# Modulation weights of the first five column blocks loaded in units of two row blocks

## Chip, cores and metric

The kernel runs on one core of a Trainium2 chip. The metric is the device time of one execution in microseconds. Before the change it was 3902.84 us, the median of 3 runs (3902.77 to 3905.11).

## What is computed

Two blocks of a diffusion-like network follow each other on 1024 latent tokens of width 1024, with 256 context tokens. The first block mixes the tokens by a Hyena long convolution and a gated linear recurrence (HGRN2), followed by a mixture of 16 experts. The second has two mixer layers with differential attention. Both blocks scale and shift their normalised inputs by modulation rows, which come from one vector for the latent tokens and one for the context:

```python
s_lat = jax.nn.silu(c)
s_ctx = jax.nn.silu(c_ctx)
sh1, sc1, g1, sh2, sc2, g2 = jnp.split((s_lat @ ada_w[l] + ada_b[l])[:, None, :], 6, axis=-1)
sh1c, sc1c, g1c, sh2c, sc2c, g2c = jnp.split(s_ctx @ ada_w[l] + ada_b[l], 6, axis=-1)
h = modulate(rmsnorm(x, norm1_g[l]), sh1, sc1)
...
shift, scale, gate = jnp.split(jax.nn.silu(c) @ w_mod + b_mod, 3, axis=-1)
shift_c, scale_c, gate_c = jnp.split(jax.nn.silu(c_ctx) @ w_mod + b_mod, 3, axis=-1)
```

So each modulation is a product of 2 rows (the two vectors) with a weight matrix of 1024 rows and 3072 or 6144 columns, all in float32.

## The kernel before

A modulation is made in column blocks of 1024 columns by `mod_rows` (line 306). For one block there are 16 products: 8 row blocks `k` of 128 rows, each in two halves `cb` of 512 columns. A product multiplies the 128x2 vectors (stationary) with a 128x512 piece of weights (moving) and gives 2 rows of 512. The four places `p0 = 64 * (k % 2) + 32 * cb` of one PSUM bank take the products of two neighbouring row blocks; each uses its own 32 columns of the array, so that products in different places can go through side by side. Two additions on VectorE and the bias complete the block. This is done for

- the first two blocks of `ada_w`, in `start` (line 742), ahead of everything that needs a normalised input. Each 128x512 piece is a load of its own (256 KB, lines of 2 KB), in a pool `mr` of 8 buffers;
- the three blocks of `w_mod_2[0]`, in `mods_layer(0)`, which runs beside the streams below with a pool `mr` of 2 such buffers;
- later blocks (`mods_tail`, `mods_layer(1)`) with 128x1024 pieces, which the change leaves as they are.

`start` also normalises the inputs, transposes them (`load_h`, line 399), runs the small network of the filter (`filter_mlp`) and projects the context (`ctx_proj`, line 777), whose weights come in 24 loads to 6 buffers `cr`.

Then `run` (line 1981) lets three streams go side by side. The first is one chain: `filter_time` (line 488; 32 steps, each of 2 matmuls into `pf`, a product with a window `H`, a sum and a difference on VectorE, an absolute value on ScalarE and a sum on GpSimd), `filter_spectra` (line 630) and `hyena` (line 898) with four long convolutions (line 652). One long convolution has 9 bins, each a forward product from `yh`, `yl` and an inverse product from `ph`, `pl`, with DFT constants `dc` that GpSimd loads (line 619). The second stream is `hy_proj` and `hg_proj`: projections of the latent tokens (`T`) with weights from `ar`, split into a high part `ah` (ScalarE) and a low part `al` (GpSimd); 1728 matmuls into `pp`. The third is `mods_layer(0)`. `ctx_state` and `hgrn_head` follow, then the context's part of the second block, the output projection, the choice of tokens and the experts.

The order on each engine isn't that of the code. A scheduler places every instruction by a model of the times, and each engine and each queue of DMAs then works strictly in the order it was given. Loads of all these tiles are issued by SP (line 177), except `dc`. A pool's buffers lie where the pool was opened: pools on one side form a stack, and a pool that is opened after others were closed takes over their space; its first tiles wait for the last readers there.

Of the kernel before, what the change touches and what calls it, by code (L numbers as in the profile page):

```python
# [22 lines left out]
D = 1024  # L23
# [107 lines left out]
class Work:  # L131
# [171 lines left out]
        self.act(s[:, :, 1], b, AF.Silu)  # L303
        return s

    def mod_rows(self, w, bias, c0, ncols, s, rows, pt, tmp, raw, wide=512):

        for b0 in range(c0, c0 + ncols, 1024):
            ps = self.ps(pt)
            for k in range(8):  # L310
                for cb in range(2):
                    if cb * 512 % wide == 0:
                        r = self.t(raw[k % len(raw)] if wide > 512 else raw, [128, wide])
                        self.dma(r, w[k * 128:k * 128 + 128, b0 + cb * 512:b0 + cb * 512 + wide])
                    p0 = 64 * (k % 2) + 32 * cb
                    self.mm(ps[p0:p0 + 2], s[:, k, :], r[:, cb * 512 % wide:cb * 512 % wide + 512], k < 2, k > 5)
            for cb in range(2):
                br = self.t(tmp, [2, 512])
                self.dma(br, bias[b0 + cb * 512:b0 + cb * 512 + 512].partition_broadcast(2))
                self.tt(br, br, ps[32 * cb:32 * cb + 2], ADD)  # L320
                self.tt(br, br, ps[64 + 32 * cb:66 + 32 * cb], ADD)
                self.dma(rows[:, b0 + cb * 512:b0 + cb * 512 + 512], br)
            yield
# [16 lines left out]
        self.m2 = self.dram([2, 2, 3 * D], name="m2")  # L340
        self.A_2, self.sh_2 = [], []

    def mods_layer(self, l, pt, tmp, raw, wide=512):

        I = self.I
        on = self.offb["norm_g_2"]
        yield from self.mod_rows(I["w_mod_2"][l], I["b_mod_2"][l], 0, 3 * D, self.scol2, self.m2[l], pt, tmp, raw, wide)
        mods = self.rows_to_cols(self.m2[l], 0, 16, pt, tmp)
        A = self.cst([128, 2, 8], name="A")
        for i in range(2):  # L350
            self.stt(A[:, i], mods[:, i, 8:16], 1.0, self.cb[:, on + l * 8:on + l * 8 + 8], ADD, MUL)
        self.A_2.append(A)
        self.sh_2.append(mods[:, :, 0:8])

    def mods_tail(self, pt, tmp, raw, wide=512):

        I = self.I
        yield from self.mod_rows(I["ada_w"][0], I["ada_b"][0], 2 * D, 4 * D, self.scol, self.ada, pt, tmp, raw, wide)
        mods = self.rows_to_cols(self.ada, 3 * D, 16, pt, tmp)
        og = self.offs["norm2_g"]  # L360
        self.A2 = self.cst([128, 8], name="A2")
        self.sh2 = mods[:, 0, 0:8]
        self.stt(self.A2, mods[:, 0, 8:16], 1.0, self.ca[:, og:og + 8], ADD, MUL)
# [1603 lines left out]
def side_by_side(*streams):  # L1967

    todo = [[-lead / total, total, list(gens)] for lead, total, gens in streams]
    while todo:  # L1970
        s = min(todo, key=lambda t: t[0])
        g, w = s[2][0]
        if next(g, todo) is todo:
            s[2].pop(0)
            if not s[2]:
                todo.remove(s)
        else:
            s[0] += w / s[1]


def run(K):
    fst = ExitStack()
    with ExitStack() as e1:
        K.open(e1, "left", ar=3, ah=4, al=4)
        K.open_ps(e1, "left", pp=3, mp=1)
        K.open(e1, "left", u2=4, T=16)
        K.open_ps(fst, "right", pf=4)
        K.open(fst, "right", f4=7, fb=5, y=2, t=3, H=2)
        with ExitStack() as e2:
            K.open(e2, "right", cr=6, x=4, c=2, mr=8)  # L1990
            K.start()
        K.open(fst, "right", yh=2, yl=2, ph=2, pl=2, dc=5, ri=7, ra=2, mr=2)
        K.mods_first()
        side_by_side((30, 450, [(K.filter_time(), 2.4), (K.filter_spectra(), 2.1), (K.hyena(), 5)]),
                   (0, 64, [(K.hy_proj(), 1), (K.hg_proj(), 1)]),
                   (0, 4, [(K.mods_layer(0, "mp", "mr", "mr"), 1)]))
    fst.close()
    with ExitStack() as cx:
        with ExitStack() as e1:
            K.open_ps(e1, "left", ph0=3, ph1=3)  # L2000
            K.open(e1, "left", hmk=1, hS=2)
            for p in "01":
                K.open(e1, "left", **{"hi" + p: 6, "hw" + p: 5, "h2" + p: 3, "hm" + p: 4, "hT1" + p: 2, "hT2" + p: 4})
            K.ctx_state()
            for h in range(4):
                K.hgrn_head(h)
            K.open(cx, "right", wr=2, wh=2, wl=2, cu=6, cv=2, Tc=4, lg=2)
            K.pfx = "c"
            with ExitStack() as e2:
                K.open_ps(e2, "right", cp=1, cm=1)  # L2010
                K.open(e2, "right", mr=1)
                for _ in K.mods_tail("cm", "cv", ("wr", "wr", "mr"), 1024):
                    pass
                K.ctx_first()
                K.ctx_side()
                for _ in K.mods_layer(1, "cm", "cv", ("wr", "wr", "mr"), 1024):
                    pass
        K.open_ps(cx, "right", cp=1, cm=1)
        K.pfx = "o"
        em = cx.enter_context(ExitStack())  # L2020
        with ExitStack() as e0:
            K.open_ps(e0, "left", pp=3, pq=2, pi=1)
            with ExitStack() as e1:
                K.open(e1, "left", xm=3, rw=1, wo=16, m4=3, yt=6, u2=3)
                K.out_proj()
            K.open(em, "left", el=4, eh=4, er=10)
            with ExitStack() as e1:
                K.open(e1, "left", twr=2, twh=2, twl=2)
                K.open(e1, "left", aff=1, tk=12, tp=2, af=4)
                K.topk()  # L2030
                K.pfx = "c"
                K.ctx_heads("tw")
        with ExitStack() as e1:
            K.open_ps(e1, "left", et=1, ea=3, ey=2)
            K.open(e1, "right", g2b=1, xg=1, xf=1, xh=4, sa=4, hh=4, yo=2)
            side_by_side((0, 64, [(K.moe(), 1)]), (CL, CT, [(K.ctx_rest(), 1)]))
    K.pfx = ""
    with ExitStack() as e1, ExitStack() as e0, ExitStack() as ec:
        K.open(e0, "right", T0=16)
        rope = K.lat_pools(ec)  # L2040
        hT = K.first_rows()
        K.lat_path(hT, rope, ec, e0, e1)


class Kern:
# [9 lines left out]
    def start(self):  # L2055
        W = self.work
        W.pc, W.psm, W.pd, W.one = self.pc, self.psm, self.pd, self.one
        run(W)
# [119 lines left out]
```

## Time and profile before

| | |
|---|---|
| median of 3 runs | 3902.84 us |
| the profiled execution | 3905.45 us |
| its span | 3903.6 us |
| TensorE busy (matmuls) | 91% |
| VectorE busy | 72% |
| ScalarE busy | 59% |
| GpSimd busy | 31% |
| read from memory, written | 712.65 MB, 107.05 MB |

The span is the time from the first to the last instruction in the profile; 1.85 us of the execution lie around it. Busy shares of the whole span average over stages with different limits, so stretches of the trace are read one by one. Matmuls are pipelined: their busy time counts as one while they overlap, and the start of the next is the better measure of what one costs. A float32 product of 512 columns is recorded as two matmuls.

### The profile page before, as it was taken

The page shows a single profiled execution, that of the slowest core. Times are in us where ns is not written, and L with a number is a line of the kernel's source. Part 1 is how long each engine was busy: PE and PEld are TensorE (multiplying, and loading weights), DVE is VectorE, ACT ScalarE, POOL GpSimd, SP SyncE. Part 2 cuts the span into 40 slices and gives each one's busy share as a digit, 9 for nine tenths or more (in the row PEclk, how much of TensorE's full clock was granted, in tenths as well). Part 3 has the DMA queues.
Part 4 walks back from the last instruction along what each step waited for, and adds up shares of the span by engine and source line. Part 5 has one row for each costly group of instructions (what it writes and reads, how often), then busy time and mean ns, then how long its engine had stood idle before and what let it go on. Part 6 is the DMA issues. An engine that isn't in the chain of part 4 may idle for free. (4 is left out here: it accounts for less than half of the span.)

```text
span 3903.6 us, 52551 instructions
## 1 busy us (share of the span) xinstructions
PE 3554.2 (91%) x17938; PEld 2859.8 (73%) x17938; DVE 2829.5 (72%) x4263; ACT 2290.4 (59%) x3733; POOL 1206.4 (31%) x844
## 2 busy tenths in 40 slices
PE   6999899768897899999999999969989899999989
PEld 2667688646766678787777777768777678877767
DVE  4587778899735788888888888855576744466662
ACT  4444433355434687777777777765566754456772
POOL 3455655454413313221111111001233520133361
PEclk7999999879998999999999999989999999999999
DMA  7767776655376699999999999962311143231133
GB/s 222 228 213 227 224 224 205 220 176 195 103 260 207 197 321 356 322 330 336 361 367 358 363 365 356 362 204 86 111 64 59 49 147 120 74 120 56 41 103 114
DMA packets 529365, 824.25 MB, mean 211 GB/s; under 512 B 38065, under 2 KB 241863, under 8 KB 529096
## 3 DMA queue, kind: packets, MB, share of 16 engines
q1 hardware_dynamic: 502024, 755.74, 56.4%
q0 software_dynamic: 26048, 64.09, 5.9%
q8 instruction: 141, 2.31, 0.2%
q10 hardware_dynamic: 1024, 1.06, 0.1%
q14 instruction: 128, 1.05, 0.1%
HBM read 712.65 MB, written 107.05 MB: 210 GB/s over the span
## 5 line engine op out<-in xcount | busy, mean ns | idle before, releaser
L187 DVE TENSOR_TENSOR el<-er,eh 128x1024 fp32r<-128x1024 f32 x763 | 950.3, 1294 | 113.9 <-ACT eh L184 110.2
L184 ACT ACTIVATE eh<-er 128x1024 fp32r<-128x1024 f32 x768 | 782.9, 1057 | 127.4 <-PE ea L206 92.3
L205 PE MATMUL ea<-el,xh 128*128 128x512 f32 x1024 | 415.5, 406 | 22.7 <-DVE el L187 20.1
L204 PE MATMUL ea<-eh,xh 128*128 128x512 f32 x1024 | 403.7, 397 | 1.0 <-ACT eh L184 0.9
L206 PE MATMUL ea<-eh,xh 128*128 128x512 f32 x1024 | 404.4, 395 | 0.0
L1284 POOL DMA_INDIRECT acc<-yo,idx x16 | 72.0, 4501 | 734.9 <-DVE yo L196 727.9
L1507 DVE TENSOR_SCALAR_CACHE_REDUCE E<-s,rq 128x512 f32<-128x512 f32 (+1 forms) x384 | 237.4, 656 | 82.9 <-PE s L209 75.3
L205 PEld LDWEIGHTS ea<-el,xh 128*128 128x128 f32 x1024 | 192.8, 188 | 91.8 <-DVE el L187 51.3
L181 ACT ACTIVATE E<-E,a 128x1280 f32<-128x1280 f32 x160 | 216.7, 1359 | 64.8 <-DVE a L1511 60.1
L209 PE MATMUL s<-KA,QA 128*128 128x512 f32 (+1 forms) x768 | 213.0, 401 | 33.0 <-DVE E L1507 32.5
L204 PEld LDWEIGHTS ea<-eh,xh 128*128 128x128 f32 x1024 | 192.8, 188 | 46.0 <-ACT eh L184 2.0
L206 PEld LDWEIGHTS ea<-eh,xh 128*128 128x128 f32 x1024 | 193.1, 189 | 37.4
L205 PE MATMUL ey<-el,hh 128*128 128x512 f32 x512 | 207.7, 406 | 4.9 <-DVE el L187 4.7
L204 PE MATMUL ey<-eh,hh 128*128 128x512 f32 x512 | 204.8, 406 | 7.5 <-ACT eh L184 7.5
L206 PE MATMUL ey<-eh,hh 128*128 128x512 f32 x512 | 204.1, 399 | 0.0
L187 POOL TENSOR_TENSOR wl<-wr,wh 128x1024 fp32r<-128x1024 f32 (+1 forms) x48 | 116.1, 2426 | 266.7 <-ACT wh L184 203.7
L209 PEld LDWEIGHTS s<-KA,QA 128*128 128x128 f32 x768 | 134.3, 202 | 76.0 <-DVE E L1507 57.8
L184 ACT ACTIVATE u<-pp 32x512 f32<-32x512 f32 (+2 forms) x212 | 124.4, 587 | 99.7 <-PE pp L206 93.5
L209 PE MATMUL po<-th,V 128*128 128x256 f32 x640 | 168.7, 389 | 15.3 <-ACT th L184 15.3
L204 PE MATMUL pp<-T,ah 128*128 128x512 f32 x448 | 180.8, 403 | 0.0
L205 PE MATMUL pp<-T,ah 128*128 128x512 f32 x448 | 177.8, 397 | 0.0
L206 PE MATMUL pp<-T,al 128*128 128x512 f32 x448 | 177.6, 397 | 0.0
(522 smaller groups left out, 9503.9 us busy)
## 6 DMA issues: line engine op xcount, KB each, us to landing
er<-in_exp_w_dram SPq DMA_DIRECT2D x768, 512.0 KB
wr<-in_w_in_dram SPq DMA_DIRECT2D x60, 512.0 KB
dc<-in_k_dft_dram POOLq DMA_DIRECT2D x72, 384.0 KB, 4.4
dc<-in_k_dft_dram POOLq DMA_DIRECT2D x72, 256.0 KB, 4.2
ar<-in_w_in_dram SPq DMA_DIRECT2D x64, 256.0 KB
mr<-in_w_mod_dram SPq DMA_DIRECT2D x48, 256.0 KB
wr<-in_ada_w_dram SPq DMA_DIRECT2D x24, 512.0 KB
wr<-in_w_out_dram SPq DMA_DIRECT2D x24, 512.0 KB
```

The costliest lines, as they stand in the source:

```text
L181: return self.nc.scalar.activation(out, in_, func, **kw)
L184: return self.nc.scalar.activation(out, in_, AF.Copy)
L187: return (eng or self.nc.vector).tensor_tensor(out, a, b, op=op)
L204: mm(out, lh, rh, start=first, stop=False)
L205: mm(out, lh, rl, start=False, stop=False)
L206: mm(out, ll, rh, start=False, stop=last)
L209: self.nc.tensor.matmul(out, l, r, start=first, stop=last)
L1284: nc.gpsimd.indirect_dma_start(out=self.acc, out_offset=x[0], in_=yo, in_offset=None, compute_op=ADD)
L1507: nc.vector.tensor_scalar(E[:, k0:k1], o, r, None, op0=MUL, op1=ALU.min, accum_out=mx[:, m, j:j + 1] if nc_ > 1 else mc)
```

## The change

In `mod_rows`, two neighbouring row blocks become one load: a tile of 128 x 2 x 1024 elements, 1 MB, with lines of 4 KB, on which four products depend (2 row blocks, 2 halves). The first five column blocks are made this way (`pair=True`): 20 loads instead of 80. Later blocks keep their 128x1024 loads (`pair=False`). The pools change for it: `mr` in `start` has 4 of the large buffers, `mr` beside the streams has one, `dc` has 4 buffers instead of 5, and `y`, `t` and `H`, which `filter_time` uses, are opened after the pools of `start` are closed instead of before.

```diff
-    def mod_rows(self, w, bias, c0, ncols, s, rows, pt, tmp, raw, wide=512):
+    def mod_rows(self, w, bias, c0, ncols, s, rows, pt, tmp, raw, pair=True):
...
             for k in range(8):
+                if not pair:
+                    r = self.t(raw[k % len(raw)])
+                    self.dma(r, w[k * 128:k * 128 + 128, b0:b0 + 1024])
+                elif k % 2 == 0:
+                    r2 = self.t(raw, [128, 2, 1024])
+                    self.dma(r2, w[k * 128:k * 128 + 256, b0:b0 + 1024].rearrange("(k p) n -> p k n", p=128))
+                if pair:
+                    r = r2[:, k % 2]
                 for cb in range(2):
-                    if cb * 512 % wide == 0:
-                        r = self.t(raw[k % len(raw)] if wide > 512 else raw, [128, wide])
-                        self.dma(r, w[k * 128:k * 128 + 128, b0 + cb * 512:b0 + cb * 512 + wide])
                     p0 = 64 * (k % 2) + 32 * cb
-                    self.mm(ps[p0:p0 + 2], s[:, k, :], r[:, cb * 512 % wide:cb * 512 % wide + 512], k < 2, k > 5)
+                    self.mm(ps[p0:p0 + 2], s[:, k, :], r[:, cb * 512:cb * 512 + 512], k < 2, k > 5)
...
-        K.open(fst, "right", f4=7, fb=5, y=2, t=3, H=2)
+        K.open(fst, "right", f4=7, fb=5)
         with ExitStack() as e2:
-            K.open(e2, "right", cr=6, x=4, c=2, mr=8)
+            K.open(e2, "right", cr=6, x=4, c=2, mr=4)
             K.start()
-        K.open(fst, "right", yh=2, yl=2, ph=2, pl=2, dc=5, ri=7, ra=2, mr=2)
+        K.open(fst, "right", y=2, t=3, H=2, yh=2, yl=2, ph=2, pl=2, dc=4, ri=7, ra=2, mr=1)
...
-                for _ in K.mods_tail("cm", "cv", ("wr", "wr", "mr"), 1024):
+                for _ in K.mods_tail("cm", "cv", ("wr", "wr", "mr"), False):
...
-                for _ in K.mods_layer(1, "cm", "cv", ("wr", "wr", "mr"), 1024):
+                for _ in K.mods_layer(1, "cm", "cv", ("wr", "wr", "mr"), False):
```

The schedule changes with it, up to the end of the HGRN2 heads and in a few places behind. Three places on TensorE follow.

The first is in the head, where the last transposes of the first 256 tokens (`x`, the identity `ident`) are followed by the context projection (`cr`, `c`). Before, steps of `filter_time` (from `fb` into `pf`) stand between them:

```order
L209 MATMUL pf_1041<-fb_998,f_99_358 128x512
L209 MATMUL pf_1057<-fb_997,f_99_358 128x512
L209 MATMUL pf_1057<-fb_998,f_99_358 128x512
L212 MATMUL pp_481<-ident_116,x_411 128x128
L212 MATMUL pp_481<-ident_116,x_413 128x128
L209 MATMUL pf_1070<-fb_997,f_99_358 128x512
L209 MATMUL pf_1070<-fb_998,f_99_358 128x512
L209 MATMUL pp_499<-cr_495,c_361 128x128 x4
```

With the change, the same place on TensorE:

```order
L212 MATMUL pp_417<-ident_107,x_354 128x128
L212 MATMUL pp_417<-ident_107,x_356 128x128
L212 MATMUL pp_424<-ident_107,x_354 128x128
L212 MATMUL pp_424<-ident_107,x_356 128x128
L209 MATMUL pp_442<-cr_438,c_304 128x128 x4
```

No filter step is left there; 32 of the 64 matmuls of `filter_time` stood ahead of the first projection matmul, and 8 do now.

The second is the change's place of these 8, right ahead of the first projection (`T` with `ah`), behind the last context unit:

```order
L212 MATMUL pp_887<-ident_107,x_826 128x128
L209 MATMUL pf_956<-fb_949,f_72_301 128x512
L209 MATMUL pf_967<-fb_949,f_72_301 128x512
L209 MATMUL pf_980<-fb_949,f_72_301 128x512
L209 MATMUL pf_993<-fb_949,f_72_301 128x512
L209 MATMUL pf_956<-fb_950,f_72_301 128x512
L212 MATMUL pp_894<-ident_107,x_824 128x128
L212 MATMUL pp_894<-ident_107,x_826 128x128
L209 MATMUL pf_967<-fb_950,f_72_301 128x512
L209 MATMUL pf_980<-fb_950,f_72_301 128x512
L209 MATMUL pf_993<-fb_950,f_72_301 128x512
L204 MATMUL pp_1169<-T_338,ah_1159 128x512
```

These are 4 steps; the other 28 come between the projections. Counted over the whole order, the first inverse product of the first long convolution (`pf` from `ph`) stood behind 1069 projection matmuls and now stands behind 1259; at the last projection matmul three long convolutions were issued, and now two are.

The third shows products of `mods_layer(0)` on TensorE (`mr` with `silu` into `mp`). Before, two of them between units of the context projection:

```order
L209 MATMUL mp_1246<-mr_1253,silu_986 2x512
L209 MATMUL pp_817<-c_361,cr_813 128x256 x4
L209 MATMUL pp_817<-c_362,cr_815 128x256 x4
L209 MATMUL mp_1246<-mr_1256,silu_986 2x512
L209 MATMUL pp_834<-c_361,cr_830 128x256 x4
```

With the change, the third unit, between projections:

```order
L206 MATMUL pp_1169<-T_345,al_1166 128x512
L209 MATMUL mp_1198<-mr_1211,silu_938 2x512 x4
L204 MATMUL pp_1272<-T_338,ah_1159 128x512
L205 MATMUL pp_1272<-T_346,ah_1159 128x512
```

Four products of one unit stand together. That is so for 6 of the 12 units of `mods_layer(0)`; the four products of each of the other 6 are issued in two parts (2 and 2, or 1 and 3) with other work between. Of these 18 groups, 4 stand ahead of the first projection matmul.

## Rows read from the trace of the kernel before

**Rows 1.** The page, busy time of engines: us, share of the span, instructions.
```profile
PE 3554.2 (91%) x17938; PEld 2859.8 (73%) x17938; DVE 2829.5 (72%) x4263; ACT 2290.4 (59%) x3733; POOL 1206.4 (31%) x844
```

**Rows 2.** Busy time by stretches, with granted clock, DMA share and rate.
```profile
core 0: us, PE busy (x) PEld busy (x) DVE busy (x) ACT busy (x) POOL busy (x), PEclk, DMA share, GB/s
0.00:47.00 47.00, 30.25 (x71) 3.46 (x71) 7.13 (x17) 4.14 (x10) 12.10 (x29) 0.75 0.91 284
47.00:81.00 34.00, 17.01 (x50) 10.14 (x51) 22.82 (x38) 28.45 (x59) 8.08 (x7) 0.55 0.40 123
81.00:157.00 76.00, 66.43 (x354) 50.83 (x353) 45.68 (x80) 38.16 (x89) 39.16 (x41) 0.92 0.74 228
157.00:511.00 354.00, 327.44 (x1720) 252.23 (x1721) 279.15 (x410) 143.05 (x302) 198.41 (x182) 0.95 0.74 224
511.00:742.00 231.00, 221.14 (x1215) 192.54 (x1214) 188.06 (x327) 80.01 (x149) 114.72 (x98) 0.98 0.66 210
742.00:804.00 62.00, 29.86 (x171) 26.93 (x170) 60.34 (x116) 21.17 (x49) 30.90 (x37) 0.72 0.71 228
804.00:1024.00 220.00, 166.63 (x1128) 134.17 (x1129) 204.16 (x337) 124.95 (x338) 120.86 (x95) 0.85 0.45 153
1300.00:2400.00 1100.00, 1060.71 (x4895) 850.55 (x4895) 960.42 (x929) 849.97 (x1051) 197.14 (x84) 0.99 0.97 341
```

**Rows 3.** Timeline of TensorE: first and last projections, first inverse product of each convolution.
```profile
156.75 0.80 PE L204 MATMUL pp<-T,ah 128*128 128x512 f32 x1
...
511.19 0.28 PE L204 MATMUL pf<-ph,dc 128*128 128x256 f32 x1
...
597.38 0.28 PE L204 MATMUL pf<-ph,dc 128*128 128x256 f32 x1
...
682.53 0.28 PE L204 MATMUL pf<-ph,dc 128*128 128x256 f32 x1
...
741.60 0.39 PE L205 MATMUL pp<-T,ah 128*128 128x512 f32 x1
741.83 0.39 PE L206 MATMUL pp<-T,al 128*128 128x512 f32 x1
...
768.66 0.41 PE L204 MATMUL pf<-ph,dc 128*128 128x256 f32 x1
```

**Rows 4.** Timeline of TensorE and the view of tile mr (100 to 500, then whole).
```profile
30.10 1.89 PE L209 MATMUL mp<-mr,silu 128*2 128x512 f32 x8
...
136.47 1.02 PE L209 MATMUL mp<-mr,silu 128*2 128x512 f32 x2
137.42 10.63 PE L209 MATMUL pp<-c,cr 128*128 128x256 f32 x48
...
148.19 1.03 PE L209 MATMUL mp<-mr,silu 128*2 128x512 f32 x4
...
L209 PE MATMUL mp<-mr,silu x96: 591/592/1061, 125.7 to 489.5; 128*2 128x512 f32 x96
...
  DMA mr<-in_ada_w_dram: 38.7, 26
```

**Rows 5.** Groups of instructions on VectorE and GpSimd, 0 to 157; one row of ScalarE's timeline.
```profile
L187 DVE TENSOR_TENSOR f<-t 128x256 f32<-128x256 f32 x32 | 20.6, 685 | 0.2
L187 DVE TENSOR_TENSOR t<-pf,H 128x512 f32<-128x512 f32 x16 | 10.8, 682 | 6.2 <-DMA H<-in_k_win_dram 4.2 <-PE pf L209 1.9
...
L187 POOL TENSOR_TENSOR fb<-fb,t 128x512 f32<-128x512 f32 x14 | 18.6, 1327 | 15.6 <-ACT t L181 15.4
...
58.60 1.28 ACT L181 ACT_TABLE_LOAD   x1
```

**Rows 6.** Who waited for whom (us, times, longest): 511 to 742; TensorE 740 to 900.
```profile
POOL dc L621 <- PE pf L206: 62.7, 30, 5.8
...
PE pf L204 <- DMA dc<-in_k_dft_dram: 4.5, 4, 1.4
```

More of the change, by code (lines that the diff above doesn't have):

```diff
@@ L341, in mods_first, with mods_layer @@
         self.A_2, self.sh_2 = [], []
-    def mods_layer(self, l, pt, tmp, raw, wide=512):
+    def mods_layer(self, l, pt, tmp, raw, pair=True):
         I = self.I
         on = self.offb["norm_g_2"]
-        yield from self.mod_rows(I["w_mod_2"][l], I["b_mod_2"][l], 0, 3 * D, self.scol2, self.m2[l], pt, tmp, raw, wide)
+        yield from self.mod_rows(I["w_mod_2"][l], I["b_mod_2"][l], 0, 3 * D, self.scol2, self.m2[l], pt, tmp, raw, pair)
         mods = self.rows_to_cols(self.m2[l], 0, 16, pt, tmp)
@@ L353, in mods_layer, with mods_tail @@
         self.sh_2.append(mods[:, :, 0:8])
-    def mods_tail(self, pt, tmp, raw, wide=512):
+    def mods_tail(self, pt, tmp, raw, pair=True):
         I = self.I
-        yield from self.mod_rows(I["ada_w"][0], I["ada_b"][0], 2 * D, 4 * D, self.scol, self.ada, pt, tmp, raw, wide)
+        yield from self.mod_rows(I["ada_w"][0], I["ada_b"][0], 2 * D, 4 * D, self.scol, self.ada, pt, tmp, raw, pair)
         mods = self.rows_to_cols(self.ada, 3 * D, 16, pt, tmp)
```

## Prediction

> **What bounds the kernel now.** The page's first view gives TensorE 91% and VectorE 72% of the span [rows 1], an average over stages, so I read the busy time by stretches next [rows 2]. The reader should see five regimes ahead of the expert stage, which the change leaves alone. To 47 us the DMA engines are the limit: 91% busy, 284 GB/s, while the first two column blocks (8.39 MB) and early inputs come in. To 81 us ScalarE is, with 28.5 of 34 us. To 157 us TensorE works 66.4 of 76 us on the context projection and the transposes. Then two streams share the engines to 742 us: the projections (1728 matmuls, the first at 156.75 us, the last at 741.83 us [rows 3]) and the filter and Hyena chain. TensorE is 92 to 96% busy there, VectorE only 79 to 81%. From 742 us it turns round: TensorE is down to 48%, VectorE up at 97%, then 93% to 1024 us.
>
> The chain ends this part, since HGRN2's remaining work and everything after waits for its last long convolution. The four convolutions show as first inverse products at 511.19, 597.38, 682.53 and 768.66 us [rows 3]: one in 86 us, always.
>
> **The change, part by part.** I follow two dates: the first projection and the last convolution.
>
> *Products.* One product is two records. Alone it takes 1.02 us, two side by side 1.03, four 1.89 at the low clock, where the head's are [rows 4]. So a slot costs the same whatever stands in it; the next work starts 0.95 us after it (136.47 to 137.42). After 100 us there are 96 records, so 48 products [rows 4], in 26 slots of one and 11 of two, 37 together. In the changed order 6 of the 12 units stay whole and 6 are cut in two, so 18 slots. That takes 19 x 0.95 = 18 us off TensorE's queue: 2 us (6 slots become 4) ahead of the first projection, 16 us (31 become 14) behind it. In the head the matrix waits for its data 38.7 us [rows 4], so fewer slots gain nothing there by themselves.
>
> *Loads.* 60 issues go, of queues that were not the limit. The lines grow from 2 to 4 KB. The nearest row with such lines is the expert stage's 341 GB/s at 97% [rows 2]. At that rate 8.39 MB take 24.6 instead of 29.5 us, 5 us less; I take 6, with the shorter wait of the last products. The ends are 0 and 8 (47 us x 284 GB/s = 13.3 MB, all at 341, is 39 us).
>
> *The filter loses its cover.* Pools y, t and H now open after the start's pools close, so they stand on the space of `cr` and `x`, and the filter's time steps cannot begin before the last context unit. Before, 16 of the 32 steps were done at 157 us: VectorE 20.6 + 10.8 us, so 1.96 us a step, GpSimd 1.33 us [rows 5]. In the changed order only 4 precede the first projection. 12 steps move: 24 us of VectorE, 16 us of GpSimd, 24 matmuls. What covered them was VectorE's idle time, 30 of the 76 us to 157. On TensorE the head gets shorter by those 24 matmuls and the 2 slots: I take 5 us of its 66.4, since some sat in gaps. Two more table loads (1.28 us each [rows 5]) cost ScalarE 2.6 us; I take 1. First projection: 156.75 - 6 - 5 + 1 = 147.
>
> *TensorE's queue to the first convolution.* Now the order decides. Before the first inverse product there stood 1069 projection matmuls, now 1259. A step is 0.23 us (741.60 to 741.83 [rows 3]). So 190 x 0.23 = 44 us come ahead of it, the 24 filter matmuls add 5.5, and the slots take 16 off: +33 us. The stretch took 354 us, 26.6 of them idle on TensorE [rows 2]; I let 8 of the idle go, because projections wait for little. 354 + 33 - 8 = 379, and 147 + 379 = 526, so 15 us later than 511. The ends: no idle time goes (+8) or all of it (-19).
>
> *The convolutions.* When the last projection is issued, two convolutions are done where it was three. Two periods of 86 us therefore stay as they were; the third now runs without projections. It can't be under 72 us: 188 us of VectorE in the 231 us to 742 [rows 2] are 70 us a period, at 97%. It need not be shorter than 86 either, as a chain waits between its engines. I take 79, so -7. The fourth's last 35 us (768.66 to 804) already ran beside no projection and stay.
>
> *Fewer buffers.* `dc` goes from 5 to 4. GpSimd waited for these buffers 30 times, 62.7 us, between 511 and 742 us [rows 6], and behind that wait stand its butterflies and the low halves of the projection weights. TensorE's own waits for them are 4 times, 4.5 us [rows 6]. I take +3, with ends 0 and 20 (one such 1.1 us for each of the 18 bins of two convolutions). `mr` is one buffer: SP's queue holds a unit's load until four products are done, and the window loads `H` behind it. +1, ends 0 and 9 (below).
>
> *Behind the last convolution* VectorE's order is the old one again, and only local swaps are left, so the shift goes through to the end at cost 0. The expert stage hides nothing of it: TensorE is 96% busy there.
>
> Sum: +15 - 7 + 3 + 1 = +12 us on a span of 3903.6 us in an execution of 3905.45 us. The median of the runs is 2.6 us lower, so 3902.84 + 12 = **3915 us**. What a measurement here can tell from no change is about 0.2%, 8 us.
>
> **Rivals.** *Break-even*: the saved slots and the faster loads pay for the lost cover. That is 12 us more: either 20 of TensorE's 26.6 us of idle time go instead of 8, or 13 of them and the third period is 72 us. For it: VectorE has 75 us idle to 511, room for the 24 that move. Against it: its waits are those of a chain. 3903 us, within 8.
>
> *Faster*: the convolutions gain once projections stand in their way less. If VectorE fills the stretch from the first inverse product to 804 us to 93%, as it does in 804 to 1024, its 248 us there (188.1 + 60.3) take 267 instead of 293; the first inverse product 15 us late then still ends 26 - 15 = 11 us ahead, and with an earlier first projection (-2) and half the idle time gone (-5) 18 us. That gives 3885 us. It decides at a VectorE share of 89% (248 in 293 - 15); the 81% to 742 us speaks against it, the 97% behind it for it.
>
> *Much slower*: a unit in one piece holds up what is queued behind it. At 224 GB/s [rows 2] 1.05 MB take 4.7 us, against 1.2 for a 256 KB piece, and in the changed order two of the units stand among the window loads of the filter steps; VectorE already waited 4.2 us for windows [rows 5]. Two such delays are 9 us, and the upper `dc` end adds 17: 3915 + 8 + 17 = 3940 us. The Trainium skill, DMA: Bandwidth & Descriptors, in "Queues, rings and completion order", says that each engine consumes a ring's descriptors in their order, so a small load cannot pass a large one ahead of it. By that rule both delays come in full; the trace has no such large load beside small ones to show it.
>
> *The change doesn't do what it says*: in part so, as 6 of 12 units are cut in two; that is in the sum. Were the other 6 cut too, that is 6 x 0.95 us more, 3921 us, inside the forecast's range.
>
> **How the numbers follow.** Forecast 0.42 (its own range 3908 to 3930), break-even 0.26, faster 0.22, much slower 0.10. So faster 0.22, same 0.26, slower 0.52. The range 3886 to 3940 leaves out about half of the faster case and half of the much slower one, some 0.16.
>
> **What would show it.** Right, if the first projection comes at 141 to 153 us with 4 filter steps ahead of it, the first inverse product near 526 us, two convolutions at the last projection (near 690 us) instead of three, and the last first inverse product near 780 us; the 48 products in about 18 slots. Wrong, if TensorE's idle share between those dates halves, if the third period falls to 72 us, or if the order behind 850 us no longer carries the shift to the end.

## The result and the profile after

Over 4 runs the changed kernel took 3935.59 us in the median (3928.3 to 3939.79), the kernel before 3903.98 us (4 runs, 3902.77 to 3908.64). The ratio is 1.0073, with a 95% interval of 1.0054 to 1.0091: slower by about 0.7%, 28 us by the ratio and 31.6 by the medians. The profiled execution of the changed kernel, 3928.3 us, is the shortest of its four; its span is 22.9 us longer than the one before.

The page answers to [rows 1]. TensorE has 26 us less to do and the kernel is slower all the same:

```profile
span 3926.5 us, 52450 instructions
PE 3528.6 (90%) x17938; PEld 2856.4 (73%) x17938; DVE 2830.2 (72%) x4263; ACT 2294.1 (58%) x3735; POOL 1196.6 (30%) x844
```

TensorE's timeline gives the dates that stand in [rows 3] for the kernel before, here the first and the last projection and the first inverse product of each of the four long convolutions (start, duration, instruction). Ahead of them stands the last group of products of the head, and between them one unit of `mods_layer(0)`, four products, and the matmul behind it:

```profile
40.60 1.89 PE L209 MATMUL mp<-mr,silu 128*2 128x512 f32 x8 [0.77 <-DMA mr<-in_ada_w_dram]
...
140.21 0.63 PE L204 MATMUL pp<-T,ah 128*128 128x512 f32 x1
...
146.43 1.04 PE L209 MATMUL mp<-mr,silu 128*2 128x512 f32 x8
147.40 0.50 PE L204 MATMUL pp<-T,ah 128*128 128x512 f32 x1
...
535.42 0.39 PE L204 MATMUL pf<-ph,dc 128*128 128x256 f32 x1 [1.48 <-ACT ph L184]
...
632.84 0.28 PE L204 MATMUL pf<-ph,dc 128*128 128x256 f32 x1
...
691.56 0.39 PE L206 MATMUL pp<-T,al 128*128 128x512 f32 x1
...
727.32 0.38 PE L204 MATMUL pf<-ph,dc 128*128 128x256 f32 x1 [2.19 <-ACT ph L184]
...
802.25 0.41 PE L204 MATMUL pf<-ph,dc 128*128 128x256 f32 x1
```

The first projection is 16.5 us earlier than before, the first inverse product 24.2 us later and the fourth convolution's 33.6 us later. To see why, I cut both traces at the same events: first projection, first inverse product, last inverse product (811.3 us before, 839.8 after). Busy time by stretches, before (the columns are those of [rows 2]):

```profile
0.00:156.75 156.75, 113.43 (x472) 64.18 (x473) 75.62 (x132) 70.75 (x157) 59.10 (x77) 0.79 0.71 221
156.75:511.20 354.45, 327.89 (x1723) 252.68 (x1723) 279.35 (x410) 143.05 (x302) 198.66 (x182) 0.95 0.74 224
511.20:811.30 300.10, 255.62 (x1408) 223.80 (x1406) 252.24 (x449) 103.35 (x201) 145.62 (x134) 0.91 0.66 209
```

and with the change, with two stretches of the head first (the clock of 1.00 in the first of them is no reading, as the last section shows):

```profile
0.00:47.00 47.00, 19.68 (x71) 2.16 (x71) 7.42 (x19) 6.71 (x15) 17.03 (x33) 1.00 0.96 321
47.00:71.00 24.00, 11.56 (x37) 5.78 (x37) 15.73 (x27) 21.00 (x45) 3.85 (x3) 0.98 0.19 58
...
0.00:140.20 140.20, 93.39 (x436) 58.77 (x437) 41.16 (x80) 65.86 (x144) 44.00 (x68) 0.94 0.64 205
140.20:535.40 395.20, 361.62 (x1947) 293.53 (x1945) 314.02 (x461) 160.40 (x334) 222.88 (x197) 0.96 0.74 225
535.40:839.80 304.40, 222.65 (x1216) 195.37 (x1217) 249.98 (x449) 95.32 (x186) 122.25 (x129) 0.85 0.63 195
```

The reader should follow VectorE (the third engine) first. Up to the first inverse product it does 355 us in both. Before, 75.6 of them lay ahead of the first projection; now only 41.2 do, so 34 us have moved into the stretch behind it. There VectorE is busy 79% of the time in both traces (279.35 of 354.45, 314.02 of 395.20), and the stretch is 40.7 us longer. TensorE gives the same 40.7 us in another way: 33.7 us more work (361.62 for 327.89) and 7 us more idle time, at 91.5% busy for 92.5%. The sum of dates is -16.5 + 40.7 + 4.3 = +28.5 us at the last inverse product. Behind it the last router product comes 30.6 us later and the first product of the expert stage 29.6; the end of these two executions is 22.9 us apart.

VectorE's groups ahead of the first projection show what is gone; the two filter groups of [rows 5], 20.6 and 10.8 us, have no row here:

```profile
L193 DVE TENSOR_SCALAR u<-pp,A,mods 128x256 f32<-128x256 f32 x16 | 8.6, 543 | 16.4 <-PE pp L212 6.8 <-POOL T L187 3.8 <-DMA dVc<-u 2.9
L196 DVE SCALAR_TENSOR_TENSOR f<-f,f 64x1024 f32<-64x1024 f32 (+1 forms) x6 | 7.4, 1230 | 0.1
L192 DVE TENSOR_SCALAR x<-x,ss 128x1024 f32<-128x1024 f32 x10 | 7.1, 748 | 0.1
L187 DVE TENSOR_TENSOR u<-u,mp 2x512 f32<-2x512 f32 x8 | 5.4, 681 | 38.7 <-PE mp L209 38.5
```

The packing itself does what it says: four products take 1.04 us, and the next matmul starts 0.97 us after their start, as behind one or two [rows 4]. The 48 products stand in 18 groups. Summed from the start of each group to the next other matmul, these are 21.1 us, where 36 groups came to 43.2 before. At 0.95 us a slot the 18 fewer groups are 17 us of that; the other 5 are idle time before the matmul behind a group.

Who waited for whom with the change: VectorE from the first projection to the first inverse product, TensorE from there to the last (us, times, longest):

```profile
DVE t L187 <- DMA H<-in_k_win_dram: 19.8, 8, 8.9
...
PE pf L204 <- DMA dc<-in_k_dft_dram: 24.0, 12, 5.6
```

VectorE's wait for windows in the same stretch before:

```profile
DVE t L187 <- DMA H<-in_k_win_dram: 0.6, 1, 0.6
```

TensorE's for `dc` was 4.5 us [rows 6]. Both look like causes; the runs below tell how far they are.

### The profile page after: what moved, and what is told of

It reads as the page before. It is cut to its first block, busy times and chain, and to the rows that moved or that the text cites. A ratio compares the mean times of both kernels' runs of the same rounds, so it can differ in the third digit from the quotient of the medians.

```text
span 3926.5 us, 52450 instructions
## 1 busy us (share of the span) xinstructions
PE 3528.6 (90%) x17938; PEld 2856.4 (73%) x17938; DVE 2830.2 (72%) x4263; ACT 2294.1 (58%) x3735; POOL 1196.6 (30%) x844
## 3 DMA queue, kind: packets, MB, share of 16 engines
q10 hardware_dynamic: 1024, 1.06, 0.1%
## 5 line engine op out<-in xcount | busy, mean ns | idle before, releaser
L205 PEld LDWEIGHTS ea<-el,xh 128*128 128x128 f32 x1024 | 192.7, 188 | 92.5 <-DVE el L187 52.3
```

What stands on the lines that cost most here:

```text
L205: mm(out, lh, rl, start=False, stop=False)
```

## The experiments

Three causes compete. **Cover:** `y`, `t`, `H` open late, so the filter's work moves behind the first projection. **Buffer:** `dc` has four buffers instead of five. **Units:** large loads in SP's queue, with one buffer. A fourth reading runs across them: each edit makes the scheduler put other numbers of projections ahead of the convolutions (order theory). The kernel before was run beside each batch: 3906.81, 3905.19 and 3902.13 us in the median.

**The late pools alone.**

```diff
-    K.open(fst, "right", f4=7, fb=5, y=2, t=3, H=2)
+    K.open(fst, "right", f4=7, fb=5)
...
-    K.open(fst, "right", yh=2, yl=2, ph=2, pl=2, dc=5, ri=7, ra=2, mr=2)
+    K.open(fst, "right", y=2, t=3, H=2, yh=2, yl=2, ph=2, pl=2, dc=5, ri=7, ra=2, mr=2)
```

> The kernel before, with nothing changed but the place where y, t and H are opened: behind the pools of start. Narrow loads and five dc buffers stay. Cover theory: 12 filter steps (24 us of VectorE) move behind the first projection. VectorE's share behind it was 81% to the last inverse product in both traces, so the stretch grows by 24/0.81 = 30 us while the head gets some 5 us shorter: 25 us over the kernel before, about 3929 us, with the first inverse product near 530 us. Buffer theory (dc) and unit theory (large loads): neither has changed here, so 3904 us within 8.

Measured: 3925.34 us, ratio 1.006 (1.0044 to 1.0075), 23 us. Busy time by stretches, cut at the same events:

```profile
146.80:540.10 393.30, 365.48 (x1908) 284.31 (x1907) 309.30 (x463) 159.43 (x330) 218.71 (x195) 0.97 0.75 227
540.10:833.60 293.50, 232.40 (x1263) 204.41 (x1263) 248.86 (x449) 96.07 (x189) 128.29 (x130) 0.87 0.65 204
```

With narrow loads and five `dc` buffers, VectorE has 30 us more behind the first projection, still 79% of a stretch that is 38.9 us longer. This is the changed kernel's long stretch, without its units: the cover alone is enough for most of the loss. The time is near the cover theory's 3929 us; the first inverse product, at 540.2 us, is 10 us behind its date.

**Four `dc` buffers alone.**

```diff
-    K.open(fst, "right", yh=2, yl=2, ph=2, pl=2, dc=5, ri=7, ra=2, mr=2)
+    K.open(fst, "right", yh=2, yl=2, ph=2, pl=2, dc=4, ri=7, ra=2, mr=2)
```

> The kernel before with four dc buffers instead of five, nothing else. Cover theory: the forecast's term, +3, so 3907 us and at most 3915. Buffer theory: this carries most of the 31 us that the change cost, so 3920 us or more, with TensorE's waits for dc behind the last projection near the 24 us of the changed kernel instead of 4.5. Unit theory: 3904 us.

Measured: 3936.22 us, ratio 1.0082 (1.0067 to 1.0096). The buffer alone costs as much as the whole change, and the forecast's +3 us fails. The waits behind it are smaller than that theory had them (13.5 us on TensorE for `dc` from the first projection to the last inverse product). Busy time by stretches, cut as before:

```profile
153.00:521.40 368.40, 342.27 (x1786) 266.21 (x1786) 274.33 (x413) 147.19 (x307) 203.26 (x186) 0.95 0.73 220
521.40:834.10 312.70, 248.84 (x1343) 216.25 (x1342) 252.88 (x446) 100.45 (x196) 138.63 (x133) 0.89 0.63 196
```

Both stretches grow, by 14 and 12.6 us, though VectorE's work in them is that of before or 5 us less. In the first it is TensorE that has 14 us more to do; in the second TensorE has 7 us less to do and 19 us more idle time. The order has 1140, 1416 and 1705 projection matmuls ahead of the first three convolutions, for 1069, 1317 and 1556.

**The change with its cover back.** For the space, `mr` in `start` has two of the large buffers instead of four.

```diff
-    K.open(fst, "right", f4=7, fb=5)
+    K.open(fst, "right", f4=7, fb=5, y=2, t=3, H=2)
...
-            K.open(e2, "right", cr=6, x=4, c=2, mr=4)
+            K.open(e2, "right", cr=6, x=4, c=2, mr=2)
...
-    K.open(fst, "right", y=2, t=3, H=2, yh=2, yl=2, ph=2, pl=2, dc=4, ri=7, ra=2, mr=1)
+    K.open(fst, "right", yh=2, yl=2, ph=2, pl=2, dc=4, ri=7, ra=2, mr=1)
```

> The changed kernel with y, t and H opened early again, as before the change; for their space mr in start has two of the large buffers instead of four. Units, dc with four buffers and the single mr buffer beside the streams stay. Cover theory: what the change cost is gone, and the loads' 6 us may show: 3895 to 3910 us, first inverse product near 505 us. Buffer theory: 3920 us or more. Unit theory: 3925 us or more, since every large load is still there, the ones beside the streams with their single buffer too.

Measured: 3906.27 us over 12 runs, ratio 1.0002 (0.9993 to 1.0011): the whole loss is gone, with four `dc` buffers and every unit in place. Busy time by the same stretches:

```profile
153.80:498.10 344.30, 320.62 (x1794) 262.71 (x1794) 274.78 (x412) 145.77 (x312) 201.66 (x187) 0.97 0.76 235
498.10:818.60 320.50, 250.16 (x1332) 218.91 (x1333) 255.59 (x447) 100.63 (x196) 130.70 (x135) 0.87 0.61 191
```

The first stretch is 51 us shorter than the changed kernel's and VectorE's work in it 39 us less. The cover theory foresaw this run, with the first inverse product at 498 for 505. The convolutions took 320 us, 20 more than before, where the theory had nothing to say.

**Units in `start` alone** (two large buffers in the place of eight small; `start`'s call of `mod_rows` gets `wide=2048`, which asks for units and isn't shown here).

```diff
-            K.open(e2, "right", cr=6, x=4, c=2, mr=8)
+            K.open(e2, "right", cr=6, x=4, c=2, mr=2)
```

> The kernel before with units of two row blocks in start alone (two large buffers in the place of eight narrow ones, the same space); the blocks beside the streams stay narrow, dc has five buffers, y, t and H open early. Cover theory: only the head's loads change, so 0 to 6 us less than before, 3898 to 3904 us, with the last product of the head near 42 us instead of 46. Unit theory: two large loads in flight keep the DMA engines less busy than eight narrow ones, and TensorE waits for whole units: 3908 us or more.

Measured: 3906.84 us over 12 runs, ratio 1.0011 (0.9999 to 1.0023): neither theory's number, no difference shown. TensorE's timeline shows waits of up to 12.33 us for a unit in the head, and its last group at 56.16 us:

```profile
41.51 1.89 PE L209 MATMUL mp<-mr,silu 128*2 128x512 f32 x8 [12.33 <-DMA mr<-in_ada_w_dram]
...
56.16 1.89 PE L209 MATMUL mp<-mr,silu 128*2 128x512 f32 x8 [0.91 <-DMA mr<-in_ada_w_dram]
```

In the changed kernel, with four such buffers, that group starts at 40.60. The head's last product record starts at 57.0 us here and at 46.0 in the kernel before, so 11 us in the loads cost 3 us at the first projection (159.9 for 156.75) and nothing that the runs can tell at the end.

**The other corners.** Four kernels complete the pairs. Units beside the streams, with `dc=4` and `mr=1` there:

```diff
-    (0, 4, [(K.mods_layer(0, "mp", "mr", "mr"), 1)])
+    (0, 4, [(K.mods_layer(0, "mp", "mr", "mr", 2048), 1)])
```

> The kernel before with four dc buffers and, beside the streams alone, units of two row blocks in one mr buffer; start's loads stay narrow, y, t and H open early. If the units beside the streams are what brought the four-buffer kernel back from 3936 to 3906 us (18 us fewer of TensorE's time in slots, and what follows from it), this comes out at 3900 to 3910 us with the first inverse product near 498 us. If that came from start's two large buffers, it stays at 3930 us or more, first inverse product near 521.

The same with `dc=5`; the space comes from a constant:

```diff
-        self.ones = self.cst([128, 128], name="ones")
+        self.ones = self.cst([128, 1], name="ones")
```

> As the run with units beside the streams alone, but with five dc buffers; half a KB for it comes from a constant of ones, of which only one column is read. Waiting theory (four buffers make TensorE and GpSimd wait for DFT constants, wherever the order puts things): the whole 29 us come off, 3875 to 3882 us. Order theory (a missing buffer costs because it puts more projections ahead of the convolutions): this order has 1117 projection matmuls ahead of the first inverse product, 48 more than the kernel before, 11 us, against 18 us of slots saved: 7 us less than before, 3900 us, with three convolutions done at the last projection. If units only repair what the lost buffer costs: 3906 us, no change.

The late pools with `dc=4` and narrow loads:

```diff
-    K.open(fst, "right", yh=2, yl=2, ph=2, pl=2, dc=5, ri=7, ra=2, mr=2)
+    K.open(fst, "right", y=2, t=3, H=2, yh=2, yl=2, ph=2, pl=2, dc=4, ri=7, ra=2, mr=2)
```

> The kernel before with y, t and H opened late and four dc buffers, narrow loads everywhere: the changed kernel without its units. If the two costs add up (19 and 29 us): 3955 us, and the units then gave 20 us of it back. If both cost through the same thing, projections ahead of the convolutions (here 1226 and 1512 ahead of the first two; 1259 and 1560 in the changed kernel): 3935 to 3942 us, near the changed kernel, and the units gave little.

And the changed kernel with `dc=5` (and the small constant):

```diff
-    K.open(fst, "right", y=2, t=3, H=2, yh=2, yl=2, ph=2, pl=2, dc=4, ri=7, ra=2, mr=1)
+    K.open(fst, "right", y=2, t=3, H=2, yh=2, yl=2, ph=2, pl=2, dc=5, ri=7, ra=2, mr=1)
```

> The changed kernel with five dc buffers instead of four (the space from the constant of ones), nothing else. Waiting theory: the 29 us of the lone lost buffer come off, 3907 us. Order theory: 1257 projection matmuls still stand ahead of the first inverse product, as with four buffers, and only the stretch between the first and the second has fewer (243 for 301, 13 us): 3922 us. Cover theory as forecast (dc counts 3 us): 3932 us.

Measured, all eight, as ratio to the kernel before with its interval:

| | five `dc` | four `dc` |
|---|---|---|
| early, narrow | 1 | 1.0082 (1.0067 to 1.0096) |
| early, units beside the streams | 0.9996 (0.9986 to 1.0006) | 1.0017 (1.0003 to 1.0031) |
| late, narrow | 1.006 (1.0044 to 1.0075) | 1.0094 (1.008 to 1.0107) |
| late, units (in `start` too) | 1.0034 (1.0021 to 1.0046) | 1.0073 (1.0054 to 1.0091), the change |

At 3904 us, 0.001 is 3.9 us, and the intervals reach 4 to 7 us to either side, so that a difference of two of these ratios under some 8 us isn't clear of zero. Opening late costs 23 and 15 us with five buffers, 5 and 22 with four. Losing the buffer costs 32, 8, 13 and 15 us. The units give 25 us back with early pools and four buffers, 8 to 10 with late ones, and with early pools and five buffers nothing that can be told from zero. The costs don't add: late pools and a lost buffer, 23 and 32 us alone, make 37 together. So in the changed kernel, with its units, the late pools are worth 22 us and the missing buffer 15 (against the corners beside it), and the two overlap. The dates say where the late pools act: the first inverse product stands at 535 to 540 us in all four late kernels and at 497 to 521 in the four early ones. Busy time from the first projection to that product in three of them (early with units and four buffers, late and narrow with four, the change with five):

```profile
148.50:497.00 348.50, 323.64 (x1794) 264.32 (x1794) 279.36 (x413) 145.98 (x312) 201.93 (x187) 0.97 0.75 233
...
142.50:537.00 394.50, 366.00 (x1907) 284.65 (x1906) 305.70 (x464) 159.10 (x331) 219.37 (x195) 0.97 0.75 228
...
137.30:539.20 401.90, 359.83 (x1949) 292.32 (x1947) 318.26 (x462) 160.23 (x334) 223.92 (x199) 0.96 0.72 221
```

In microseconds the four medians, in the order of the runs above, were 3912.51, 3902.9, 3938.36 and 3919.08. The first is 2.5 us above its range, with its first inverse product at 497.0 us for 498. The second ends the waiting theory for `dc`, which wanted 3875 to 3882; it lies between the order theory's 3900 and no change, and doesn't tell these apart. The third is no sum of the two costs, and the fourth is nearest to the order theory's 3922.

The count of projections ahead doesn't give the date by itself, though. With early pools and four buffers 1140 of them stood ahead of the first inverse product without units and 1148 with units beside the streams, and it came at 521.4 and 497.0 us. The slots' time behind the first projection, summed as above with the idle time in it, was 40.4 us and 24.7, which is 16 of these 24 us. The granted clock of the stretch read 0.95 and 0.97; on some 340 us of TensorE that would be 7 us more, an estimate.

**Three window buffers in the changed kernel** (and the small constant).

```diff
-    K.open(fst, "right", y=2, t=3, H=2, yh=2, yl=2, ph=2, pl=2, dc=4, ri=7, ra=2, mr=1)
+    K.open(fst, "right", y=2, t=3, H=3, yh=2, yl=2, ph=2, pl=2, dc=4, ri=7, ra=2, mr=1)
```

> The changed kernel with three buffers for the windows H instead of two (the space again from the constant of ones). Its order is nearly the same: 1264 and 1550 projection matmuls ahead of the first two convolutions, for 1259 and 1560. In the changed kernel VectorE waited 19.8 us for windows behind the first projection, 7 to 9 with narrow loads at the same late place. Window theory (large loads in the same queue delay the small window loads, and that is why the units gained little there): the wait falls below 8 us, the first inverse product comes 12 us earlier, near 523 us, and the time is 3922 to 3926 us. Order theory (only what stands ahead on TensorE counts): 3935 us within 5, first inverse product near 535 us, whatever VectorE waits for.

VectorE's waits with three buffers, from the first projection to the first inverse product:

```profile
DVE t L187 <- DMA H<-in_k_win_dram: 9.8, 3, 4.1
```

The wait is half of the changed kernel's 19.8 (a wait for another load into `H`, from `Hd`, rose from 0.6 to 4.8 us), and the time stays: 3935.26 us, ratio 1.0082 (1.0069 to 1.0095), first inverse product at 535.7 us. The waits for windows were plain to see in the trace, and the 10 us of them that went were not what set the end; what the rest costs no run shows. The first projection even came 7.2 us earlier (133.0 us), and that too bought nothing. The stretch between the two:

```profile
132.90:535.70 402.80, 364.92 (x1948) 295.30 (x1946) 317.01 (x464) 161.72 (x336) 221.90 (x199) 0.96 0.72 223
```

**Six `dc` buffers** in the kernel before, first alone, then with the chain further ahead.

```diff
-    K.open(fst, "right", yh=2, yl=2, ph=2, pl=2, dc=5, ri=7, ra=2, mr=2)
+    K.open(fst, "right", yh=2, yl=2, ph=2, pl=2, dc=6, ri=7, ra=2, mr=2)
```

> The kernel before with six dc buffers instead of five, nothing else; it has 1069, 1304 and 1548 projection matmuls ahead of the first three convolutions, where it had 1069, 1317 and 1556. From the first to the last inverse product it took 292 to 300 us with five buffers in the runs so far, 304 to 320 with four. If GpSimd's waits for a free buffer cost time at five as at four: 280 to 290 us for that stretch and 3890 to 3897 us in all. If five already cover the transfers: 3905 us, the stretch 295 to 300 us.

```diff
-        side_by_side((30, 450, [(K.filter_time(), 2.4), (K.filter_spectra(), 2.1), (K.hyena(), 5)]),
+        side_by_side((100, 450, [(K.filter_time(), 2.4), (K.filter_spectra(), 2.1), (K.hyena(), 5)]),
```

> As with six dc buffers, and the chain is given a lead of 100 instead of 30 in side_by_side, so that its steps stand further ahead: 1046, 1275 and 1521 projection matmuls ahead of the first three convolutions, and 36 filter matmuls ahead of the first projection. Order theory: 27 matmuls fewer ahead of the third are 6 us, so 6 us less than with six buffers alone, 3890 to 3899 us. If VectorE's work behind the first projection sets the end and not the order: the same time as with six buffers alone, within 3 us.

Measured: 3894.06 us, 0.9978 (0.9968 to 0.9988), and 3888.05 us, 0.9959 (0.9946 to 0.9972). A sixth buffer still pays, some 8 us. Busy time from the first to the last inverse product, with six buffers alone and with the lead:

```profile
510.00:800.20 290.20, 256.30 (x1407) 223.72 (x1405) 255.81 (x449) 101.41 (x200) 135.89 (x134) 0.94 0.68 215
...
503.00:805.10 302.10, 263.68 (x1429) 228.80 (x1429) 259.72 (x449) 102.58 (x203) 147.36 (x134) 0.93 0.66 207
```

Alone the stretch is 10 us shorter than before, with the lead 2 us longer, though both have six buffers (the second is the longest of its five executions, 3898.79 us). So the shorter stretch isn't shown to be the buffer's doing. The intervals of the two times overlap, so the lead's 6 us aren't shown either.

**A version that beats both.** Units beside the streams, five `dc`, early pools, narrow `start`, the small constant, and a longer lead:

```diff
-        side_by_side((30, 450, [(K.filter_time(), 2.4), (K.filter_spectra(), 2.1), (K.hyena(), 5)]),
+        side_by_side((60, 450, [(K.filter_time(), 2.4), (K.filter_spectra(), 2.1), (K.hyena(), 5)]),
```

> Units of two row blocks beside the streams, five dc buffers, y, t and H open early, start's loads narrow (as the run that came out at 3902.9 us), and the chain's lead in side_by_side 60 instead of 30. Ahead of the convolutions stand 1095, 1352 and 1617 projection matmuls, for 1117, 1354 and 1599. Order theory: 5 us less to the first inverse product and nothing behind it, as the third has 18 more ahead: 3898 to 3904 us. A version that beats the kernel before by over 0.2% would be under 3897 us.

Measured: 3875.55 us (3873.18 to 3882.95), ratio 0.9931 (0.9919 to 0.9943), 27 us better than the kernel before. Busy time by stretches of its profiled execution (3882.95 us, the longest of its six):

```profile
152.20:488.10 335.90, 308.42 (x1734) 253.44 (x1733) 277.73 (x405) 142.84 (x302) 198.67 (x182) 0.96 0.76 234
488.10:792.20 304.10, 250.01 (x1382) 218.01 (x1381) 257.05 (x450) 101.27 (x199) 133.67 (x136) 0.90 0.65 206
```

The first stretch is 28 us shorter than that of the same kernel with a lead of 30:

```profile
150.30:514.40 364.10, 325.02 (x1775) 267.12 (x1775) 284.94 (x417) 146.11 (x309) 198.46 (x187) 0.93 0.73 222
```

With the longer lead TensorE is busy 17 us less and idle 12 us less. Of the 17, 22 projections are 5 and 4 filter matmuls 1; the products of `mods_layer(0)` take 15.5 to 15.7 us in both. The granted clock of the stretch read 0.93 with a lead of 30 and 0.96 with 60, and 0.03 of 325 us would be some 10 us more, an estimate that no run isolates. The order theory had counted the 5 alone, so it fell short in size. Of the 27 us, 25 came with the longer lead (0.9996 to 0.9931). Whether the units have a part in them stays open: the lead wasn't run without units on five buffers.

## Why the prediction was right, and where its terms were off

The direction stands, and so does the cause that the forecast was built on: slower, because the filter loses its cover. Putting the cover back takes the loss away, and taking it away alone makes 23 of some 30 us. It isn't the whole cause: the missing `dc` buffer, which I had priced at 3 us, costs 32 alone, and giving it back takes half of the loss away.

The size, +12 for a measured +31.6 by medians, was too small. 3935.6 us lies outside the forecast's own 3908 to 3930; the wider range holds it because it reaches into the case of the rival "much slower", and that is luck. In dates, the first projection came 7 us earlier than forecast, the stretch to the first inverse product took 16 us more, and the stretch behind it changed by +4.3 us for a forecast -3: together +28.5 for +12. Of the signs named, 4 filter steps, 18 slots and two convolutions at the last projection came; the first projection (140.2), the first inverse product (535 for 526) and the last convolution's (802 for 780) missed. Step by step:

*Products.* "18 slots" held (from 36, where I had 37), and TensorE's slots fell by 22 us, 17 of them the slots themselves, for 18 forecast. That a slot costs the same for one product or four held too.

*Loads.* 6 us; the last group of the head starts at 40.60 us with the change, and the head's last product record starts at 41.4 us for 46.0 and ends at 42.5 for 46.6. That is 4 to 5 us, a little less than forecast.

*First projection.* 147 us forecast, 140.2 measured. The head's middle stage, where ScalarE is the limit, took 24 us (47 to 71) instead of 34 (47 to 81), ScalarE busy 21.0 for 28.45. The late pools alone, with narrow loads, already bring its end to 73.0 us. I had only charged ScalarE, with +1. The change's gain in the head was larger than forecast, and it bought nothing: the first inverse product didn't follow it.

*Cover.* "12 steps move: 24 us of VectorE" was the step that counted wrongly. The order put 4 steps on TensorE ahead of the first projection, but immediately ahead, so that VectorE reached none of them by then: 16 steps and 34 us moved.

*TensorE's queue to the first inverse product.* The queue's sum was right: 327.4 + 33 forecast, 361.62 measured. "I let 8 of the idle go" failed: idle time went from 26.6 to 33.6 us. That is 15 of the 16 us by which the stretch was longer than 379. VectorE's row would have given no worse a forecast: at 79% busy, 34.7 us more of it are 44 us more of stretch (40.7 measured). But it isn't shown to be the better measure. TensorE's share gives 36 us (33.7 at 92.5%), and over the eight corners it is as steady, 89 to 93%, as VectorE's, 77 to 80% in seven of them and 74% with four buffers and narrow loads. With the longer leads VectorE's was 81 and 83%. Why idle time grew by 7 us instead of shrinking by 8 stays open.

*Convolutions.* "Two periods of 86 us stay" failed: they were 97.4 and 94.5. The order had 301 projection matmuls between the first two first inverse products instead of 248, and 53 x 0.23 = 12 us is about the first one's excess of 11. I had counted the projections ahead of the first convolution and not those between. It isn't shown to be that: in the changed kernel with five `dc` buffers 243 stood between, and the period was still 92.3 us. The second had fewer, 168 for 239, and its excess of 9 us was gone with the fifth buffer (81.6 us). The third, at 74.9, was close to its 79.

*`dc`.* +3, bounded by 0 and 20: the change with five buffers was 16 us faster, and the buffer alone cost 32. I had sized it by TensorE's 4.5 us of waits [rows 6], which say little of what a lost buffer costs: they rose to 24.0 with the change, but to 13.5 only where the lost buffer cost 32. There the order changed as well, with 71 more projections ahead of the first convolution, some 16 us at 0.23 each; so the term lacked the order.

*`mr`, one buffer.* The waits for windows rose to 19.8 us, above the 0 to 9, as the rival "much slower" had it; the half of them that went with three `H` buffers was no cost. The Trainium skill, DMA: Bandwidth & Descriptors, "Queues, rings and completion order", has a ring's descriptors consumed in their order on each engine; the longer waits (9.0 us with the late pools and narrow loads, 19.8 with the units) agree with it, and no run here put the units in another queue to show it.

*Behind the last convolution.* "Cost 0" held within what the runs can tell: +28.5 us at the last inverse product, +22.9 in the profiled spans, +31.6 in the medians.

Of the rivals, "faster" and "break-even" needed more of VectorE or less idle time on TensorE, and neither came. "Much slower" (3940 us) came nearest in number: its `dc` part, 20 us in all, is near the 16 us that the fifth buffer gives back; the loads that it was named for were not shown to cost anything, and the rest of the loss is cover and order, which it didn't price. That is luck too.

## What to carry to other kernels

When work moves past an event, price the stretch behind it twice: by what is added to the busiest engine's queue, and by the moved work of the next engine at that engine's share there. Here the two gave 36 and 44 us, and 41 came; neither alone is shown to set the length. Time saved on one engine ahead of the event may buy nothing, as the earlier first projections did. A pool that is opened later moves all the work that uses it, and an order shows only when an instruction is issued, not what its successors on other engines have done by then. Before trading a buffer for space, take it away alone, and don't add up costs measured one by one: 23 and 32 us made 37 together. Look for half a KB in a constant first.

## What the runs showed of the hardware beyond that

Loads of 1 MB were not faster than loads of 256 KB by themselves. In the head, to 47 us, eight small ones in flight moved 284 GB/s [rows 2], two units, as many bytes, 275 (the run with units in `start` alone), and four units 321:

```profile
0.00:47.00 47.00, 15.97 (x55) 1.98 (x55) 5.61 (x16) 6.66 (x14) 15.85 (x32) 1.00 0.87 275
```

Each figure is that of one execution, with the other loads of the stretch in it. The Trainium skill, DMA: Bandwidth & Descriptors, "Bandwidth", asks for at least 1 MiB in a load; with two such buffers the measurement differs.

I had put the head's 1.89 us for four products down to a low clock [rows 4], and the trace of the kernel before bears it out. Its granted clock was 1.00 (2.4 GHz) from 10 to 18 us and 0.50 (1.2 GHz) from 26 to 44 us. TensorE's products of tile `mr` in these two windows (busy, clock, DMA share, rate; then the length of a record, shortest, median and longest in ns):

```profile
10.00:18.00 8.00, 5.29 (x15) 1.00 0.98 331
26.00:44.00 18.00, 8.04 (x23) 0.50 1.01 299
...
L209 PE MATMUL mp<-mr,silu x15: 591/592/592, 9.7 to 15.1; 128*2 128x512 f32 x15
...
L209 PE MATMUL mp<-mr,silu x23: 1012/1057/1061, 25.5 to 43.6; 128*2 128x512 f32 x23
```

With the change all 64 records of the head are of the slow kind:

```profile
L209 PE MATMUL mp<-mr,silu x64: 1009/1036/1061, 7.3 to 41.4; 128*2 128x512 f32 x64
```

The views print a clock of 1.00 there, as in the row of the two units above, but the changed kernel's trace has no record of the clock before 66.5 us, and a stretch without a record is printed as 1.00. So a clock at the start of a trace is worth checking against the length of a known instruction.
